# One transfer per token tile for the query and key scratch, reversed bias rows without copies, and a table chain cut into pieces

## The chip, the cores and the metric

The kernel runs on one core of one Trainium2 chip. The metric is the device time of one execution in microseconds. Three runs of the kernel before took 4225.74, 4232.83 and 4234.1 us; the median is 4232.83 us.

## What is computed

A sequence of 1024 tokens of width 1024 goes through two blocks in float32. The first block has two hybrid layers, the second one even layer and one odd layer, each followed by a wide MLP and a gated embedding step. Only the parts below touch the change:

```python
def hybrid_layer(x, c, layer_idx, ...):          # twice
    h = rms_norm(x, norm_g) * (1.0 + scale) + shift
    proj = h @ w_in                              # MLA latents, na q/k/v, diff q/k/v, gates
    o_mla = blocked_attention(q, k, v_mla, ...)  # 6 heads, 1024 x 1024 scores
    o_na = neighborhood_attention(qn, kn, vn, na_rpb, ...)   # 6 heads of 64, window 8 x 16, bias table
    o_d = blocked_diff_attention(qd, kd, vd, lam, ...)       # 4 heads, two score maps of 32 each
    return x + gate * (concat(o_mla * silu(g), ...) @ w_out)

def even_mixer(h, ...):                          # once
    q, k, v = split(rms_norm_2(h, ln) @ w_in)
    sb = stick_breaking_attention(q, k, v)       # 8 heads of 64, causal
    s5 = s5_mixer(u, ...)                        # state-space scan; needs tables of exp, cos, sin, powers
    return concat(s5, sb) @ w_out
```

## The kernel before

The program is a list of stages. Each stage has items (mostly one per token tile of 128 tokens, or one per query tile of a head) and a list `prep` of steps that are called, evenly spread, between the items of the stage ahead of it (`Net.run`, L186). A planner then orders the instructions of each engine by its own simulation of time; the order of one engine's queue is fixed after that.

**Stages of a hybrid layer**, in order: `lat`, `gate1`, `gate0`, `dv`, `dqk`, `nq`, `nk`, `nv` (projections by weight columns), then 4 stages of differential attention (`diff`), 6 of neighbourhood attention (`na`), 6 of MLA, then `out0` and `out1`. In the profile, layer 0 has `dv` to `nv` at 246 to 483 us, diff at 483 to 625, na at 625 to 730; layer 1 has them at 1165 to 1350, 1350 to 1491 and 1491 to 1597. The even layer follows `out1` of layer 1 with stages `v0`, `u`, `v1`, `q0`, `q1`, `k0`, `k1`, `glu`, and stick-breaking attention (`sb`, 8 heads) at 2189 to 2371 us.

**All data transfers are issued by SyncE's one queue** (`dma`, L243 to L249), in its order. Each issue takes one of eight completion lanes in turn, and an issue waits until the transfer that had its lane eight issues earlier has landed, as well as for the SBUF page that it writes.

**SBUF** is a pool of 43 pages of 4 KB per partition (`page`) and 10 half pages (`half`). A tile's slot is free when its last reader is done.

**Queries and keys go through DRAM.** `head_turn` (L512) transposes a token tile to features on partitions, splits it into a high and a low part on ScalarE and VectorE, and stores it into scratch laid out per head with the high rows above the low rows (`nq [6, 128, S]`, `dq [8, 64, S]`). For each group, each head of a 128-row block and each of the two parts it issues one transfer: 16 for a token tile of `dqk`, 4 for one of `nq`, `nk`, `sbq`, `sbk`. Later the attention stages load a head: `nqA`, `nqB` twice 64 rows each (L940 to L945, L1575 to L1579), `nkS` 128 rows, `dqT` four times 32 rows, `dkT` twice 64 rows (L1027 to L1033). A row is 1024 floats, 4 KB, and each loaded tile is 128 rows, 512 KB.

**The bias of the neighbourhood attention** (`na_bias`, L920): a zero-filled table `R` of 17 rows of 127 per head is written, the 15 x 31 biases are put into it, and the table is copied 64 times into `E` (3238.5 KB). The copy reads with the pattern 6 heads, 64 repeats, 2159 floats. `na_stages` (L951) then reads a Toeplitz tile `Bt` out of the copies, and GpSimd subtracts it from a mask (L961).

**The tables of the state-space mixer** (`s5_tables`, L1181): 8 steps of small VectorE instructions on 128 x 16 tiles, then 4 groups of 5 steps (`step_m` ... `step_k`) which make and store the large tables. The 8 steps and the first group stand in the prep of `out1` of layer 1, so they run beside `out0`; the other three groups stand in the preps of `v0`, `u` and `v1`.

**The modulation rows of the next layer** (`ada_steps`, L417) are made beside `dqk` to `nv` of layer 0: 32 loads of 512 KB, products on VectorE (L433), and a matmul per half row (L447).

Of the kernel before, what the change touches and what calls it, by code (L numbers as in the profile page):

```python
# [161 lines left out]
class Net:  # L162
# [23 lines left out]
    def run(self, stages):  # L186
# [18 lines left out]
        while self.active:  # L205
            self.step(None)

# [413 lines left out]
    def qk_item(self, t, hT, W, cols, heads, dst):  # L621

        def f():
# [15 lines left out]
            self.head_turn(x.rearrange("p h d -> p (h d)"), t, [hd[0:3] for hd in heads], dst)  # L639
# [32 lines left out]
    def project1(self, i, hT, early=None):  # L672
# [4 lines left out]
            "nq": [6, 128, S], "nk": [6, 128, S], "nv": [NT, 128, 768],  # L677
            "dq": [8, 64, S], "dk": [8, 64, S], "dv": [NT, 128, 256], "g": [8, 128, S]}.items()}
# [58 lines left out]
        stages.append(Stage([gains2] + W.steps(), qk(W, 512, heads((0, 8, 32, "dq", True), (256, 8, 32, "dk", True)), [D["dq"], D["dk"]]), "dqk"))  # L737
        W = self.weights(w_in[:, 416:800], 384)
        stages.append(Stage(W.steps(), qk(W, 384, heads((0, 6, 64, "nq", False)), [D["nq"]]), "nq"))
        W = self.weights(w_in[:, 800:1184], 384)  # L740
        stages.append(Stage(W.steps(), qk(W, 384, heads((0, 6, 64, "nk", False)), [D["nk"]]), "nk"))
# [3 lines left out]


# [173 lines left out]
    def na_bias(self, i):  # L920


        R = self.scratch([6, 17, 127], name=f"rpb{i}")
        E = self.scratch([6, 64, 17 * 127], name=f"rpe{i}")

        def f():
            z = self.half(F32, (128, 128), name="rz")
            self.nc.gpsimd.memset(z, 0.0)
            self.dma(R.rearrange("h j x -> (h j) x"), z[0:102, 0:127])
            self.dma(R[:, 1:16, 48:79], self.I["na_rpb"][i])  # L930
            r = R[:]
            src = bass.AP(tensor=r.tensor, offset=r.offset, ap=[[17 * 127, 6], [0, 64], [1, 17 * 127]])
            self.dma(E, src)
        return f, E

    def na_stages(self, D, mixT, E):
        nc = self.nc

        def loads(h, T):
            def q():  # L940
                T["a"] = self.page(F32R, (128, S), name="nqA")
                T["b"] = self.page(F32R, (128, S), name="nqB")
                for e in range(2):
                    self.dma(T["a"][e * 64:e * 64 + 64], D["nq"][h, 0:64])
                    self.dma(T["b"][e * 64:e * 64 + 64], D["nq"][h, 64:128])  # L945

            def k():
                T["k"] = self.page(F32R, (128, S), name="nkS")
                self.dma(T["k"], D["nk"][h])

            def b():  # L951
                Bt = T["Bt"] = self.page(F32, (128, 16, 64), name="Bt")
                r = E[:]
                for e in range(2):
                    self.dma(Bt[e * 64:e * 64 + 64], bass.AP(
                        tensor=r.tensor, offset=r.offset + h * 64 * 2159 + (1 - e) * 127 + 63,
                        ap=[[2158, 64], [127, 16], [1, 64]]))
# [45 lines left out]
    def diff_stages(self, i, D, mixT):  # L1003
# [101 lines left out]
    def block1(self):  # L1105
# [34 lines left out]
        for i in range(2):  # L1140
# [3 lines left out]
            st[3].prep.append(nf)  # L1144
# [36 lines left out]
    def s5_tables(self, T):  # L1181
# [56 lines left out]
        def exact_exp(out, x):  # L1238
# [6 lines left out]
            V.tensor_scalar_mul(out, v("r"), 1.0 / 5040)  # L1245
            for c in (1.0 / 720, 1.0 / 120, 1.0 / 24, 1.0 / 6, 0.5, 1.0):
                V.scalar_tensor_tensor(out, out, c, v("r"), op0=ALU.add, op1=ALU.mult)
            V.tensor_scalar(v("n"), v("n"), 127.0, 8388608.0, op0=ALU.add, op1=ALU.mult)
# [12 lines left out]
        def circle():  # L1261
            exact_exp(v("dt"), v("ldt"))
# [5 lines left out]
            V.scalar_tensor_tensor(v("r"), v("n"), -7.54978995489188216e-8, v("r"), op0=ALU.mult, op1=ALU.add)  # L1268
            V.tensor_mul(v("r2"), v("r"), v("r"))
# [678 lines left out]
```

## Time and profile before

| | us |
|---|---|
| median of three runs | 4232.83 |
| the profiled execution | 4231.62 |
| its span, first to last instruction | 4229.8 |
| TensorE busy | 3939.2 (93%) |
| VectorE busy | 2611.0 (62%) |
| ScalarE busy | 1815.3 (43%) |
| GpSimd busy | 1829.0 (43%) |
| differential attention, both layers | 142 + 141 |
| neighbourhood attention, both layers | 105 + 106 |
| stick-breaking attention | 182 |

The profile is of one execution. A stretch is read by the busy time of each engine in it, by the TensorE clock that was granted, and by the share of time for which the 16 DMA engines were busy. SyncE issues only, so it never counts as busy; what it does is read from its own timeline.

### The profile page before, as it was taken

Reading aid. Unit: us, or ns where it says so; the run is one execution under the profiler, and the core shown is the slowest. Engines: PE = TensorE matmul, PEld = TensorE weight load, DVE = VectorE, ACT = ScalarE, POOL = GpSimd, SP = SyncE. Lnnn points to the kernel's source line nnn. Section 1 sums busy time; section 2 is a strip of 40 time slices with the busy share of each in tenths; the row PEclk is TensorE's granted clock in tenths of the full one; section 3 lists DMA queues with packets and bytes.
Section 4 is the critical chain, followed back from the end, with each engine's and each line's share of the span. In section 5 each row is a group of like instructions: output and inputs, shape, how many; then the busy total and the mean of one; then the engine's idle time right before and its main releaser. Section 6 shows DMA issues by size and latency. Waiting matters only on the chain.

```text
span 4229.8 us, 60207 instructions
## 1 busy us (share of the span) xinstructions
PE 3939.2 (93%) x21519; PEld 3360.2 (79%) x21519; DVE 2611.0 (62%) x5073; ACT 1815.3 (43%) x3819; POOL 1829.0 (43%) x1512
## 2 busy tenths in 40 slices
PE   7996889999998899989987899999999899999999
PEld 6875658989887579878876778888888878888879
DVE  6766678846654788883669644454566744455573
ACT  5632478745534787522355331111126621111145
POOL 3432376454432774602336534444433244444432
PEclk9998999999999999999888999999999999999999
DMA  5454725332537353335453311111111111111111
GB/s 176 143 210 125 205 61 148 92 117 94 172 112 191 75 132 102 117 133 169 126 143 86 105 40 48 48 50 55 45 50 51 46 45 45 50 51 55 55 40 56
DMA packets 383549, 408.78 MB, mean 97 GB/s; under 512 B 75619, under 2 KB 311811, under 8 KB 382482
## 3 DMA queue, kind: packets, MB, share of 16 engines
q1 hardware_dynamic: 383250, 404.93, 32.5%
q8 instruction: 171, 2.80, 0.3%
q14 instruction: 128, 1.05, 0.1%
HBM read 302.86 MB, written 108.62 MB: 97 GB/s over the span
## 4 chain that ended last, share of the span: by engine, by line
PE 66%; DVE 10%; POOL 4%; ACT 4%; issue 3%; DMA 1%; SPq 0%; POOLq 0%; DVEq 0%; ACTq 0%
PE S L258 29%; PE mm L258 14%; PE tp L258 8%; PE tp L776 3%; PE mm L798 3%; PE S L914 3%; PE mm L802 1%; POOL P L761 1%; DVE P L753 1%; DVE sba L1610 1%; DVE PTl L267 1%; PE tp L337 1%; POOL wl L263 1%; PE S L1040 1%; POOL P L1612 1%
## 5 line engine op out<-in xcount | busy, mean ns | idle before, releaser
L263 POOL TENSOR_TENSOR wl<-wr,wh 128x1024 fp32r<-128x1024 f32 (+4 forms) x262 | 605.5, 2317 | 1283.0 <-ACT wh L262 822.6
L258 PE MATMUL S<-hT,wh 128*128 128x512 f32 x2176 | 688.5, 390 | 2.8 <-DVE h L1860 1.1
L1730 DVE TENSOR_TENSOR h<-h,mm 128x512 f32<-128x512 f32 x512 | 351.8, 687 | 514.8 <-PE mm L258 514.6
L258 PE MATMUL S<-wh,hT 128*128 128x256 f32 (+3 forms) x2304 | 567.9, 331 | 28.2 <-ACT vst L654 16.3
L262 ACT CAST wh<-wr 128x1024 fp32r<-128x1024 f32 (+4 forms) x264 | 262.4, 1000 | 512.7 <-PE tp L258 245.8
L258 PEld LDWEIGHTS S<-hT,wh 128*128 128x128 f32 x2176 | 407.7, 188 | 89.5 <-ACT hT L266 1.5
L1730 DVE TENSOR_TENSOR h<-h,tp 128x512 f32<-128x512 f32 x512 | 351.8, 687 | 164.7 <-PE tp L258 164.7
L258 PEld LDWEIGHTS S<-wh,hT 128*128 128x128 f32 x2304 | 411.5, 197 | 43.7 <-ACT vst L654 17.4
L258 PE MATMUL S<-hT,wl 128*128 128x512 f32 x1088 | 423.8, 389 | 1.2 <-POOL wl L263 1.1
L258 PE MATMUL S<-wl,hT 128*128 128x256 f32 (+3 forms) x1152 | 378.1, 328 | 0.7 <-POOL wl L263 0.7
L1714 ACT ACTIVATE z<-S 128x512 f32<-128x512 f32 x128 | 69.6, 596 | 634.1 <-PE S L258 634.1
L776 PE MATMUL tp<-c,P 128*128 128x128 f32 x2000 | 299.2, 286 | 36.4 <-POOL P L1612 17.1
L761 POOL TENSOR_SCALAR P<-P,sx 128x1024 f32<-128x1024 f32 (+2 forms) x232 | 232.4, 1007 | 193.7 <-DVE sx L757 90.2
L776 PEld LDWEIGHTS tp<-c,P 128*128 128x128 f32 x2000 | 240.8, 146 | 85.3 <-POOL P L1612 21.2
L267 DVE TENSOR_TENSOR PTl<-tp,PTh 128x512 fp32r<-128x512 f32 (+3 forms) x432 | 251.2, 607 | 72.3 <-ACT PTh L266 67.9
L753 DVE CUSTOM_DVE_ANT_1 P<-S,zero 128x1024 f32<-128x1024 f32 x224 | 266.8, 1216 | 32.8 <-PE S L1040 31.4
L756 ACT ACTIVATE P<-P,sx 128x1024 f32<-128x1024 f32 x224 | 258.6, 1159 | 49.6 <-DVE sx L753 36.6
L266 ACT CAST PTh<-tp 128x512 fp32r<-128x512 f32 (+3 forms) x432 | 215.2, 528 | 110.7 <-PE tp L776 104.0
L258 PE MATMUL S<-wh,mx 128*128 128x512 f32 x768 | 243.5, 394 | 3.3 <-POOL mx L819 2.6
L258 PEld LDWEIGHTS S<-hT,wl 128*128 128x128 f32 x1088 | 204.2, 188 | 44.1 <-POOL wl L263 2.0
L258 PEld LDWEIGHTS S<-wl,hT 128*128 128x128 f32 x1152 | 227.2, 197 | 6.3 <-POOL wl L263 1.0
L258 PE MATMUL mm<-wh,hT 128*128 128x256 f32 x1152 | 221.6, 285 | 2.1 <-DVE hT L267 1.7
(604 smaller groups left out, 9350.5 us busy)
## 6 DMA issues: line engine op xcount, KB each, us to landing
wr<-in_w_mlp_up_dram SPq DMA_DIRECT2D x64, 512.0 KB
wr<-in_w_mlp_down_dram SPq DMA_DIRECT2D x64, 512.0 KB
adw<-in_ada_w_dram SPq DMA_DIRECT2D x48, 512.0 KB
h<-h SPq DMA_DIRECT2D x32, 512.0 KB
wr<-in_w_in_dram SPq DMA_DIRECT2D x28, 512.0 KB
wr<-in_w_in_dram SPq DMA_DIRECT2D x24, 384.0 KB
mqT<-mq SPq DMA_DIRECT2D x24, 384.0 KB
mkT<-mk SPq DMA_DIRECT2D x24, 384.0 KB
```

The source lines that it names most:

```text
L258: self.nc.tensor.matmul(ps, a, b, start=(i == 0), stop=(i == n - 1))
L262: self.nc.scalar.copy(hi, src)
L263: (eng or self.nc.gpsimd).tensor_sub(lo, src, hi.bitcast(F32))
L266: self.nc.scalar.copy(hi, ps)
L267: self.nc.vector.tensor_sub(lo, ps, hi.bitcast(F32))
L753: nc.vector.tensor_tensor_reduce(P.rearrange("p (a b) -> p a b", a=2), Sv, self.zero.unsqueeze(2).to_broadcast([128, 2, 512]), 1.0, 3.0e38 ...
L756: nc.scalar.activation(P, P, AF.Exp, bias=nm[:, 0:1], scale=-1.0, accum_out=nm[:, 1:2])
L761: self.nc.gpsimd.tensor_scalar(P, P, f, g, op0=ALU.mult, op1=ALU.mult)
L776: self.nc.tensor.transpose(tp[:, j, :], P[:, b * 128:b * 128 + 128], self.eye)
L798: self.nc.tensor.matmul(*m, start=(j == 0), stop=(j == len(mms) - 1))
L914: nc.tensor.matmul(sp[:, c, :], T["mq", a][0:96, qs], T["mk", b][0:96, c * 512:c * 512 + 512], start=(j == 0), stop=(j == 2))
L1730: nc.vector.tensor_add(H[t][:, sl], H[t][:, sl], o)
```

## The change

1. `head_turn` stores a whole token tile with one transfer. The scratch is laid out part first: `[2, n, 128, S]` (part, block of 128 feature rows, row, token). `dq` and `dk` share one scratch `dqk [2, 4, 128, S]`.
2. A new helper `head_rows` loads a head's tile of 128 rows. Its source pattern leads with a dimension of 2 that steps from part to part (or by 0, where the same part is wanted twice). There is one transfer of 128 rows for a head of 64, and two of 64 rows for a head of 32.
3. The bias rows are reversed by a small GpSimd instruction and written to `R`; the 64 copies are gone, `Br` is read out of `R` with overlapping rows, and the subtraction reads it reversed into a page of its own.
4. The 8 table steps of the state-space mixer become 51 pieces that are mixed into the preps of `dqk`, `nq`, `nk` and `nv` of layer 1; the first group of large tables moves to the prep of the first diff stage, the second to `out1`, the third to `v1` and the fourth to `q0`.

```diff
-    def head_turn(self, x, t, groups, dst):
-        n = sum(nh * d for _, nh, d in groups) // 128
+    def head_turn(self, x, t, n, dst):
...
-        o = self.page(F32R, (128, 2, 4, 128), name="hT_")
-        self.split_ps(o[:, 0, 0:n, :], o[:, 1, 0:n, :], p[:, 0:n, :])
-        for (c0, nh, d), dd in zip(groups, dst):
-            per, b0, nb = 128 // d, c0 // 128, nh * d // 128
-            dv = dd.rearrange("(n e) (w r) s -> e w r n s", e=per, w=2)[..., t * 128:t * 128 + 128]
-            for e in range(per):
-                for w in range(2):
-                    self.dma(dv[e, w], o[e * d:e * d + d, w, b0:b0 + nb, :])
+        o = self.page(F32R, (128, 2, n, 128), name="xT")
+        self.split_ps(o[:, 0], o[:, 1], p[:, 0:n, :])
+        self.dma(dst[:, :, :, t * 128:t * 128 + 128].rearrange("w n p s -> p (w n) s"), o.rearrange("p w n s -> p (w n) s"))
...
-            "nq": [6, 128, S], "nk": [6, 128, S], "nv": [NT, 128, 768],
-            "dq": [8, 64, S], "dk": [8, 64, S], "dv": [NT, 128, 256], "g": [8, 128, S]}.items()}
+            "nq": [2, 3, 128, S], "nk": [2, 3, 128, S], "nv": [NT, 128, 768],
+            "dqk": [2, 4, 128, S], "dv": [NT, 128, 256], "g": [8, 128, S]}.items()}
...
+    def head_rows(self, src, h, d, ws, name):
+        x = self.page(F32R, (128, S), name=name)
+        per = 128 // d
+        v = src[0, h // per, h % per * d:h % per * d + d, :]
+        step = src.ap[0][0]
+        for j in range(0, len(ws), 2):
+            self.dma(x[j * d:j * d + 2 * d], bass.AP(
+                tensor=v.tensor, offset=v.offset + step * ws[j], ap=[[step * (ws[j + 1] - ws[j]), 2]] + [list(q) for q in v.ap]))
+        return x
...
-            self.dma(R[:, 1:16, 48:79], self.I["na_rpb"][i])
-            r = R[:]
-            src = bass.AP(tensor=r.tensor, offset=r.offset, ap=[[17 * 127, 6], [0, 64], [1, 17 * 127]])
-            self.dma(E, src)
-        return f, E
+            x = self.half(F32, (128, 2, 31), name="rz")[0:90]
+            self.dma(x[:, 0, :], self.I["na_rpb"][i].rearrange("h j x -> (h j) x"))
+            self.nc.gpsimd.tensor_scalar(x[:, 1, :], x[:, 0, ::-1], 1.0, 0.0, op0=ALU.mult, op1=ALU.add)
+            self.rrow = x
+        def g():
+            self.dma(R[:, 1:16, 48:79], self.rrow[:, 1, :])
+        return [f, g], R
...
-                T["a"] = self.page(F32R, (128, S), name="nqA")
-                T["b"] = self.page(F32R, (128, S), name="nqB")
-                for e in range(2):
-                    self.dma(T["a"][e * 64:e * 64 + 64], D["nq"][h, 0:64])
-                    self.dma(T["b"][e * 64:e * 64 + 64], D["nq"][h, 64:128])
+                T["a"], T["b"] = [self.head_rows(D["nq"], h, 64, w, n) for w, n in (((0, 0), "nqA"), ((1, 1), "nqB"))]
...
-                T["k"] = self.page(F32R, (128, S), name="nkS")
-                self.dma(T["k"], D["nk"][h])
+                T["k"] = self.head_rows(D["nk"], h, 64, (0, 1), "nkS")
...
-                Bt = T["Bt"]
-                nc.gpsimd.tensor_sub(Bt, self.nam.unsqueeze(1).to_broadcast([128, 16, 64]), Bt)
+                Bt = T["Bt"] = self.page(F32, (128, 16, 64), name="Bt")
+                nc.gpsimd.tensor_sub(Bt, self.nam.unsqueeze(1).to_broadcast([128, 16, 64]), T.pop("Br")[:, :, ::-1])
...
-                q = T["q", s] = self.page(F32R, (128, S), name="dqT")
-                k = T["k", s] = self.page(F32R, (128, S), name="dkT")
-                for e in range(2):
-                    self.dma(q[e * 32:e * 32 + 32], D["dq"][2 * h + s, 0:32])
-                    self.dma(q[64 + e * 32:96 + e * 32], D["dq"][2 * h + s, 32:64])
-                    self.dma(k[e * 64:e * 64 + 64], D["dk"][2 * h + s])
+                T["q", s] = self.head_rows(D["dqk"], 2 * h + s, 32, (0, 0, 1, 1), "dqT")
+                T["k", s] = self.head_rows(D["dqk"], 8 + 2 * h + s, 32, (0, 1, 0, 1), "dkT")
...
+                for j in range(4):
+                    st[4 + j].prep = self.mixed(st[4 + j].prep, tb[j * len(tb) // 4:(j + 1) * len(tb) // 4])
+                df[0].prep += steps[0]
...
-                so[1].prep += tb + steps[0]
-                self.s5_later = [("v0", steps[1]), ("u", steps[2]), ("v1", steps[3])]
+                so[1].prep += steps[1]
+                self.s5_later = [("v1", steps[2]), ("q0", steps[3])]
...
-        out = [load, turn, turn_c, circle, powers, bbar, turns, apowers]
+        def parts():
+            for part in (circle, powers, bbar, turns, apowers):
+                yield from part()
+                yield
+        gen = parts()
+        out = [load, turn, turn_c] + [lambda: next(gen, None) for _ in range(47)] + [lambda: [None for _ in gen]]
```

The stick-breaking stages load `nqA`, `nqB` and `nkS` with `head_rows` in the same way.

## Rows read from the trace of the kernel before

**Rows 1.** The page: busy time, share of the span, instructions; shares of the last chain.

```profile
PE 3939.2 (93%) x21519; PEld 3360.2 (79%) x21519; DVE 2611.0 (62%) x5073; ACT 1815.3 (43%) x3819; POOL 1829.0 (43%) x1512
...
PE 66%; DVE 10%; POOL 4%; ACT 4%; issue 3%; DMA 1%; SPq 0%; POOLq 0%; DVEq 0%; ACTq 0%
```

**Rows 2.** Windows: stretch, length, busy PE, PEld, DVE, ACT, POOL, clock, DMA share, GB/s.

```profile
246.00:290.00 44.00, 34.48 (x182) 29.01 (x181) 23.28 (x26) 16.88 (x33) 18.74 (x8) 0.88 0.97 344
349.00:404.00 55.00, 19.12 (x114) 18.21 (x112) 25.46 (x37) 10.46 (x25) 9.84 (x7) 0.72 0.46 137
...
1165.00:1180.00 15.00, 8.26 (x51) 7.85 (x49) 4.58 (x10) 7.46 (x14) 5.16 (x3) 0.77 1.03 321
1250.00:1290.00 40.00, 33.43 (x174) 31.79 (x172) 16.00 (x41) 12.84 (x33) 13.24 (x10) 0.87 0.36 90
...
1785.00:1825.00 40.00, 29.61 (x142) 24.38 (x141) 39.11 (x268) 1.44 (x3) 0.00 (x0) 0.81 0.20 65
```

**Rows 3.** Windows of the diff, na and sb attention stretches, same columns.

```profile
483.00:625.00 142.00, 121.27 (x547) 76.28 (x546) 110.88 (x211) 107.16 (x195) 108.35 (x70) 0.90 0.41 106
625.00:730.00 105.00, 98.41 (x686) 83.26 (x685) 81.76 (x224) 86.52 (x199) 69.38 (x79) 0.98 0.56 144
...
1350.00:1491.00 141.00, 118.21 (x540) 73.95 (x538) 108.20 (x208) 105.85 (x192) 106.68 (x69) 0.94 0.43 111
1491.00:1597.00 106.00, 99.44 (x701) 84.16 (x701) 85.30 (x228) 88.52 (x203) 71.36 (x81) 1.00 0.57 144
...
2189.00:2371.00 182.00, 134.44 (x803) 117.43 (x802) 168.82 (x212) 103.81 (x194) 126.56 (x132) 0.85 0.38 95
```

**Rows 4.** DMA issues by tile: count and size of one.

```profile
dqT<-dq SPq DMA_DIRECT2D x64, 128.0 KB
...
rpe<-rpb SPq DMA_DIRECT2D x2, 3238.5 KB
...
nkS<-nk SPq DMA_DIRECT2D x12, 512.0 KB
```

**Rows 5.** Windows: wide loads, the bias copy twice, and mixed traffic; columns as above.

```profile
10.00:30.00 20.00, 19.59 (x54) 12.57 (x55) 14.46 (x14) 12.94 (x13) 0.00 (x0) 1.00 1.02 407
...
1144.00:1148.00 4.00, 4.00 (x23) 3.34 (x22) 2.91 (x9) 2.56 (x8) 0.00 (x0) 1.00 0.36 147
1148.00:1152.00 4.00, 4.00 (x19) 3.33 (x18) 3.73 (x6) 1.12 (x3) 3.54 (x5) 1.00 0.37 158
...
490.00:530.00 40.00, 34.20 (x153) 21.06 (x152) 34.52 (x67) 30.89 (x56) 34.78 (x23) 0.93 0.70 178
```

**Rows 6.** Timeline of SyncE's queue: start, length of the issue in us, what, count.

```profile
223.45 9.49 SPq L248 DMA_DIRECT2D mk<-mTl  x1
232.99 8.39 SPq L248 DMA_DIRECT2D g<-gate  x1
...
337.85 3.67 SPq L248 DMA_DIRECT2D dq<-hT__3260  x8
...
1330.68 1.00 SPq L248 DMA_DIRECT2D dqT<-dq  x2
```

**Rows 7.** Issues of one tile on SyncE: ns min/median/max, first and last start.

```profile
L248 SPq DMA_DIRECT2D dqT<-dq x64: 302/419/1147, 452.9 to 1393.4; - x64
...
L248 SPq DMA_DIRECT2D nqA<-sbq x16: 450/587/3278, 2169.8 to 2313.1; - x16
L248 SPq DMA_DIRECT2D nq<-hT__3563 x4: 592/603/636, 382.4 to 384.5; - x4
```

**Rows 8.** Waits by total: waiting engine and line, releaser, us, times, longest.

```profile
PE mm L447 <- DVE acc L442: 38.8, 3, 32.9
...
PE S L258 <- ACT vst L654: 16.3, 4, 8.6
```

**Rows 9.** Waits of SyncE's own queue.

```profile
SPq L248 <- PE tp L776: 198.6, 45, 12.2
```

**Rows 10.** One line's instructions: ns min/median/max, first and last start.

```profile
L961 POOL TENSOR_TENSOR Bt<-c,Bt x12: 2375/2400/3316, 589.8 to 1574.1; 128x1024 f32<-128x1024 f32 x12
...
L1240 DVE TENSOR_SCALAR s5s<-s5s x2: 174/7391/14608, 1767.9 to 1786.8; 128x16 f32<-128x16 f32 x2
```

More of the change, by code (lines that the diff above doesn't have):

```diff
@@ L206, in run, with mixed @@
             self.step(None)
+    @staticmethod
+    def mixed(a, b):
+        k = sorted([((j + 0.5) / len(a), 0, j) for j in range(len(a))] + [((j + 0.5) / len(b), 1, j) for j in range(len(b))])
+        return [(a, b)[w][j] for _, w, j in k]
     def note(self, tag, t):
@@ L638, in f @@
             yield
-            self.head_turn(x.rearrange("p h d -> p (h d)"), t, [hd[0:3] for hd in heads], dst)
+            self.head_turn(x.rearrange("p h d -> p (h d)"), t, nall * d // 128, dst)
         return f
@@ L736, in project1 @@
         W = self.weights(w_in[:, 1568:2080], 512)
-        stages.append(Stage([gains2] + W.steps(), qk(W, 512, heads((0, 8, 32, "dq", True), (256, 8, 32, "dk", True)), [D["dq"], D["dk"]]), "dqk"))
+        stages.append(Stage([gains2] + W.steps(), qk(W, 512, heads((0, 8, 32, "dq", True), (256, 8, 32, "dk", True)), D["dqk"]), "dqk"))
         W = self.weights(w_in[:, 416:800], 384)
-        stages.append(Stage(W.steps(), qk(W, 384, heads((0, 6, 64, "nq", False)), [D["nq"]]), "nq"))
+        stages.append(Stage(W.steps(), qk(W, 384, heads((0, 6, 64, "nq", False)), D["nq"]), "nq"))
         W = self.weights(w_in[:, 800:1184], 384)
-        stages.append(Stage(W.steps(), qk(W, 384, heads((0, 6, 64, "nk", False)), [D["nk"]]), "nk"))
+        stages.append(Stage(W.steps(), qk(W, 384, heads((0, 6, 64, "nk", False)), D["nk"]), "nk"))
         W = self.weights(w_in[:, 1184:1568], 384)
@@ L923, in na_bias @@
         R = self.scratch([6, 17, 127], name=f"rpb{i}")
-        E = self.scratch([6, 64, 17 * 127], name=f"rpe{i}")
         def f():
@@ L1143, in block1 @@
             nf, E = self.na_bias(i)
-            st[3].prep.append(nf)
+            st[3].prep += nf
             stages += st
@@ L1261, in circle @@
         def circle():
-            exact_exp(v("dt"), v("ldt"))
+            yield from exact_exp(v("dt"), v("ldt"))
+            yield
             V.tensor_mul(v("th"), v("li"), v("dt"))
@@ L1268, in circle @@
             V.scalar_tensor_tensor(v("r"), v("n"), -7.54978995489188216e-8, v("r"), op0=ALU.mult, op1=ALU.add)
+            yield
             V.tensor_mul(v("r2"), v("r"), v("r"))
@@ L1271, in circle @@
             V.scalar_tensor_tensor(v("s"), v("s"), 1.0, v("r"), op0=ALU.add, op1=ALU.mult)
+            yield
             horner(v("c"), v("r2"), (-1.0 / 3628800, 1.0 / 40320, -1.0 / 720, 1.0 / 24, -0.5))
             V.tensor_scalar_add(v("c"), v("c"), 1.0)
+            yield
             V.tensor_scalar(v("q"), v("n"), -1.5, 0.25, op0=ALU.add, op1=ALU.mult)
@@ L1282, in circle @@
             V.tensor_scalar(v("even"), v("odd"), -1.0, 1.0, op0=ALU.mult, op1=ALU.add)
+            yield
             for out, a, b, op in (("sin", "s", "c", ALU.add), ("cos", "c", "s", ALU.subtract)):
@@ L1305, in powers @@
             V.tensor_mul(v("x2"), v("lr"), v("dt"))
-            exact_exp(v("mag"), v("x2"))
+            yield from exact_exp(v("mag"), v("x2"))
+            yield
             V.tensor_mul(v("ar"), v("mag"), v("cos"))
@@ L1312, in powers @@
             V.tensor_mul(rho, rho, rho)
+            yield
             square(v("p0r"), v("p0i"), v("cos"), v("sin"))
@@ L1316, in powers @@
             square(v("p0r"), v("p0i"), v("p0r"), v("p0i"))
+            yield
             unit(v("p0r"), v("p0i"))
             for m in range(1, 7):
+                yield
                 square(v(f"p{m}r"), v(f"p{m}i"), v(f"p{m - 1}r"), v(f"p{m - 1}i"))
@@ L1340, in bbar @@
             V.tensor_mul(v("fr"), v("fr"), v("den"))
+            yield
             V.tensor_mul(v("fi"), v("ai"), v("lr"))
@@ L1344, in bbar @@
             V.tensor_mul(v("fi"), v("fi"), v("den"))
+            yield
             B = P["B"] = P["bc"][:, 0]
@@ L1356, in grow @@
                 cmul(V, e[:, 0, :, m:2 * m], e[:, 1, :, m:2 * m], e[:, 0, :, 0:m], e[:, 1, :, 0:m], y[0], y[1], [w[:, 0, :, 0:m], w[:, 1, :, 0:m]])
+                yield
         def turns():
@@ L1365, in turns @@
                 V.memset(x[:, 1, :, 0:1], 0.0)
-            grow(e, w, 16, "p", 0)
-            grow(f, w, 8, "p", 4)
+            yield
+            yield from grow(e, w, 16, "p", 0)
+            yield from grow(f, w, 8, "p", 4)
         def apowers():
@@ L1376, in apowers @@
                 cmul(V, e[:, 0, :, m + 1], e[:, 1, :, m + 1], e[:, 0, :, m], e[:, 1, :, m], v("ar"), v("ai"), [w[:, 0], w[:, 1]])
+                yield
         def outer(s, out, x, y, op_r, op_i, order):
@@ L1574, in q @@
             def q():
-                T["a"] = self.page(F32R, (128, S), name="nqA")
-                T["b"] = self.page(F32R, (128, S), name="nqB")
-                for e in range(2):
-                    self.dma(T["a"][e * 64:e * 64 + 64], D["q", h // 4][h % 4, 0:64])
-                    self.dma(T["b"][e * 64:e * 64 + 64], D["q", h // 4][h % 4, 64:128])
+                T["a"], T["b"] = [self.head_rows(D["q", h // 4], h % 4, 64, w, n) for w, n in (((0, 0), "nqA"), ((1, 1), "nqB"))]
             def k():
-                T["k"] = self.page(F32R, (128, S), name="nkS")
-                self.dma(T["k"], D["k", h // 4][h % 4])
+                T["k"] = self.head_rows(D["k", h // 4], h % 4, 64, (0, 1), "nkS")
             return [q, k]
@@ L1622, in even_stages @@
         w_in = I["w_in_even_2"][0]
-        D = {(x, c): self.scratch([4, 128, S], name=f"sb{x}{c}") for x in "qk" for c in range(2)}
+        D = {(x, c): self.scratch([2, 2, 128, S], name=f"sb{x}{c}") for x in "qk" for c in range(2)}
         D["v"] = self.scratch([NT, 128, 1024], name="sbv")
@@ L1638, in mk @@
             def mk(t):
-                return lambda: self.qk_item(t, hT, W, 256, [(0, 4, 64, L[key], False)], [D[key, c]])()
+                return lambda: self.qk_item(t, hT, W, 256, [(0, 4, 64, L[key], False)], D[key, c])()
             return [mk(t) for t in range(NT)]
```

9 lines of the change are left out of this document (5 added, 4 removed).

## The prediction

> **What bounds the kernel now.** I read the page first: TensorE is busy 93% of the span and carries 66% of the last chain; no DMA, no queue and no other engine comes near [rows 1]. So an edit pays only where TensorE idles, and costs wherever it opens a new gap. The windows show the gaps near the edits [rows 2]: 35.9 of 55 us idle at 349:404 (clock 0.72), 9.5 of 44 at 246:290, 6.7 of 15 at 1165:1180, 6.6 of 40 at 1250:1290, 10.4 of 40 at 1785:1825. Then the three attentions that read the new scratch [rows 3]: diff 142 and 141 us, na 105 and 106, sb 182. They are full for TensorE or VectorE, and DMA is at 0.38 to 0.57 of sixteen engines. That spare DMA time is the cover under which every head's queries and keys are loaded, and it is what I test the change against.
>
> **Stores.** A `dqk` token tile now takes 16 issues; eight of them fill 3.67 us of SyncE, 0.46 us each [rows 6], and one of `nq` takes 0.60 us [rows 7]. Per layer 128 + 64 issues go to 24, about 59 + 38 us of queue time down to 11. What stood behind them is paid only where TensorE waited:
> - The modulation row at 371 us: TensorE waits 32.9 us for a VectorE sum [rows 8] whose 512 KB loads queue among these stores. VectorE, pages and DMA bandwidth stay, so I take two thirds of the idle 35.9 us: **-24** (0 to -36).
> - 1250:1290 in layer 1: **-5** (0 to -7).
> - sb's stores: no wait of TensorE's behind them is in my rows; nothing.
>
> **Bias copy.** After `rpe<-rpb` the next two issues block SyncE for 9.49 and 8.39 us [rows 6], and TensorE's projections wait for `vst` tiles, whose stores stand in that queue: 16.3 us over four waits, 8.6 the longest [rows 8]. Without the copies I take **-14** (0 to -16). New are a 90 x 31 GpSimd instruction and a reversed read in the subtraction. The latter took 2.4 us forward [rows 10]; reversed it may take anything from that to double, 12 x 2.4 = 29 us in all, on a GpSimd that is busy 69 of 105 us [rows 3] and a head ahead: nothing, and up to 2.4 us per layer if the first head's is late. `Br` beside `Bt` takes one page more per head.
>
> **Table chain.** In 1785:1825 VectorE is busy 39.1 of 40 us on it while TensorE idles 10.4 us at a clock of 0.81 [rows 2]. Moved into `dqk` to `nk`, where VectorE has 24 of 40 us free (1250:1290) and the pieces are under 1 us each, the head norms behind a piece lose about that much. One first instruction took 14.6 us for no reason that a row tells [rows 10]; if that recurs among the head norms it eats the gain. **-14** (0 to -16). Its loads and 11 stores move to SyncE's queue at `dqk` and `nv`; three of its pages stay allocated through the attentions.
>
> Gains together: -57 (-14, the copies alone, to -75).
>
> **Loads: the term that decides.** Before, `dqT` came as four transfers of 32 rows, `nkS` as one of 128 rows [rows 4]; the source patterns led with 32, 64 or 128. Now each leads with 2. What a short leading dimension does is seen in the bias copy, whose source leads with 6: while it runs nearly alone the DMA share is 0.36 and 0.37, that is 6/16 = 0.375, at 147 and 158 GB/s; loads with 128 leading rows fill the share to 1.02 at 407 GB/s [rows 5]. Both are 25 GB/s per busy engine (147/(16 x 0.36) = 25.5; 407/(16 x 1.02) = 24.9). I read it as: as many engines as the leading dimension has room for. With 2 that is two engines, and a 512 KB tile costs 262,144 B / 25 GB/s = **10.5 us** of both. Bounds: 10.3 (25.5 GB/s) and 16.5 (0.70 at 178 GB/s, 15.9 each [rows 5], but that traffic holds rows of 256 and 512 B, these are 4 KB rows as in the first); I take the near end, and 13 as the price that I still think likely.
>
> That SyncE sat 9.49 us on the issue behind the copy [rows 6] speaks for one line in which such loads stand behind each other. No row shows two of them in flight. The Trainium skill, "DMA: Bandwidth & Descriptors", section "Why a DMA increments its semaphore by 16 and not by 1", says that the engine count is the largest number up to 16 that divides both patterns' slowest dimensions, and that SyncE's transfers use the lowest-numbered engines; the trace agrees on the count for 6 (0.36 to 0.37). By its second half all these loads would queue on one pair, +367 as below; if each took another pair it would be the third rival's +30.
>
> Sum per stretch, loads in a stream, with the pair's share of the wide transfers (per diff head some 0.5 MB: 1.5 us; na 1.3 MB: 5; sb 0.5 MB: 2):
> - diff head: 4 x 10.5 + 1.5 = 43.5, four heads 174, against 35 us per head now. na head: 3 x 10.5 + 5 = 36.5, six heads 219, against 17.5. sb head: 33.5, eight heads 268, against 22.8.
> - Layer 0: the first issue is at 452.9 [rows 7]; 452.9 + 174 + 219 + the last head's compute 17.5 = 863, where na ends at 730 now: **+133**. Layer 1 from 1330.7 [rows 6]: 1741 against 1597: **+144**. sb from 2169.8 [rows 7]: 2461 against 2371: **+90**. Together +367.
> - SyncE waits for pages that TensorE frees (`SPq <- PE tp L776`, 45 times [rows 9]); where the next na head's first load waits for the present head's compute, the pair runs dry for some 4 us a head: **+50** for both layers (0 to +100).
>
> Queued behind a narrow load on SyncE stand the `nv` and `nk` stores, `V`, gates, and everything eight issues later by its lane; TensorE waits for these only through the loads already counted. That SyncE does block behind a copy on few engines is seen in the 9.49 us issue [rows 6].
>
> 4231.6 (profiled execution) + 367 + 50 - 57 = **4592 us**. The profiled execution is 1.2 us under the median of three, which I ignore.
>
> **Rivals.**
> 1. *The clock falls in the gaps as well.* Granted 0.72 where TensorE idled most [rows 2]. At half clock diff's busy time would be 121.3 x 0.90/0.5 = 218 us, over the stream's 174 (layer 1: 118.2 x 0.94/0.5 = 222); na's 193 and sb's 228 stay under. +92: 4684. Against: TensorE would be busy 0.7 of the time in diff, and sb ran at 0.85 with that share [rows 3].
> 2. *The pattern isn't carried as written* and the loads use all sixteen engines: in each part the 64 (or 32) rows are one contiguous run, and contiguous runs do load wide now. Then only the gains are left: 4231.6 - 57 = 4175, faster. For it: `nkS` lands in time today. Against: the bias copy also reads contiguous rows and kept its 6. It decides once the share in na stays near 0.5 and the stage near 105 us.
> 3. *Each narrow load gets another pair.* Up to eight in flight then hide each other, and only the first head of the five or so unhidden starts waits some 6 us longer: 4231.6 - 57 + 30 = 4205, faster. Against: SyncE sat 9.49 us on one issue behind the copy [rows 6] while the share left ten of sixteen engines idle [rows 5], so a queue in order doesn't flow around a narrow transfer.
>
> **How the numbers follow.** Forecast 0.79, rival 1 0.08, rival 2 0.08, rival 3 0.03, and 0.02 for gains and costs that cancel. Predicted: 4592. Low end: the wide transfers' share hidden in the other engines' time (-12 -60 -16 = -88), no page lag (-50), full gains (-18): 4436. High end: 92 loads at 13 instead of 10.5 us (+230), lag +50: 4872; with all at 16.5 it would be over 5200, which I leave out, as I do rivals 2 and 3. Range 4430 to 4870, rival 1 within. Faster by over 0.2% 0.11, within 0.2% 0.02, slower 0.87; 0.2% is the spread of the runs before and about what can be told from no change.
>
> **What would show it.** Right: in na and sb windows a DMA share near 2/16 = 0.125 with TensorE idle, waits of the score matmuls (L977, L1040, L1594) on the `nq`, `dqk`, `sbq` loads, long issues on SyncE; na near 230 us, diff near 175, sb near 270, and no 9 us issue after the bias rows. Gains: under 15 us idle at the modulation row; `out0` of layer 1 as short as layer 0's. Wrong: if the attentions keep their lengths, the leading 2 doesn't confine the loads, and all of the +417 is void; if they grow by twice as much, the price per row was 16.5, not 10.5.

## The result, and the profile after

The changed kernel takes 4518.09 us (median; 4515.83 to 4521.76), the kernel before 4230.95 us beside it: a ratio of 1.068, 95% interval 1.066 to 1.070. It is slower by 287 us. The forecast was 4592 us, range 4430 to 4870. The profiled execution took 4517.0 us, with a span of 4515.1 us at a mean granted clock of 0.935 (before 0.965).

The page of the changed kernel, the same lines as [rows 1]: busy time, share of the span and instructions of each engine, then the shares of the last chain.

```profile
PE 3966.7 (88%) x21519; PEld 3380.7 (75%) x21519; DVE 2606.3 (58%) x5073; ACT 1815.2 (40%) x3819; POOL 1816.5 (40%) x1514
...
PE 49%; DMA 8%; DVE 4%; issue 2%; ACT 2%; POOL 2%; SPq 1%; POOLq 0%; DVEq 0%; ACTq 0%
```

TensorE does the same 21519 matmuls, but transfers, 1% of the chain before, now carry 8% of it. The waits by total (waiting engine and line, releaser, us, times, longest) say which ones:

```profile
PE S L985 <- DMA nkS<-nk: 128.5, 8, 21.0
...
PE S L1617 <- DMA nkS<-sbk: 108.9, 8, 22.7
...
PE S L1044 <- DMA dkT<-dqk: 43.1, 4, 16.4
```

Before, no score matmul waited for a load in the list of waits. L985, L1617 and L1044 are the score matmuls of na, sb and diff. The windows of the attentions answer to [rows 3] (stretch, length, busy PE, PEld, DVE, ACT, POOL, clock, DMA share, GB/s); the last three are short pieces of the first na:

```profile
433.00:616.00 183.00, 126.70 (x561) 77.86 (x560) 104.30 (x211) 110.51 (x200) 108.46 (x71) 0.84 0.24 81
616.00:815.00 199.00, 105.01 (x675) 90.56 (x673) 82.74 (x222) 84.92 (x194) 65.19 (x78) 0.75 0.30 86
...
2403.00:2654.00 251.00, 134.06 (x794) 117.33 (x795) 162.62 (x207) 99.52 (x189) 113.16 (x129) 0.76 0.20 68
620.00:630.00 10.00, 8.53 (x55) 6.46 (x53) 5.45 (x14) 7.30 (x16) 10.00 (x8) 1.00 0.13 51
655.00:670.00 15.00, 14.78 (x85) 10.90 (x84) 7.84 (x21) 9.27 (x22) 2.84 (x4) 0.91 0.13 52
640.00:650.00 10.00, 0.00 (x0) 0.00 (x0) 0.00 (x0) 0.00 (x0) 0.00 (x0) 0.50 0.28 79
```

The stages are 41, 94 and 69 us longer with the same work in them. Where only head loads are in flight the DMA share is 0.13, two of sixteen engines (0.125), at 51 to 52 GB/s, some 25 GB/s per engine; and in 640:650 no engine computes at all. The queue that issues it all, SyncE's timeline (start, length of the issue in us, what), shows the loads of one na head:

```profile
579.31 0.92 SPq L254 DMA_DIRECT2D nqA<-nq  x1
580.33 0.80 SPq L254 DMA_DIRECT2D nqB<-nq  x1
581.22 8.63 SPq L254 DMA_DIRECT2D nkS<-nk  x1
589.94 9.67 SPq L254 DMA_DIRECT2D V<-nv  x1
599.78 10.86 SPq L254 DMA_DIRECT2D gt<-g  x1
610.74 4.33 SPq L254 DMA_DIRECT2D Br<-rpb  x2
615.16 3.29 SPq L254 DMA_DIRECT2D nqA<-nq  x1
```

From one head's `nqA` to the next are 35.9 us here, and (761.2 - 579.3)/5 = 36.4 us on average over the stage. SyncE is held for some 10 us each on the issues of the wide `V` and `gt`, which stand behind the narrow loads. At the modulation row, where 35.9 of 55 us were idle [rows 2], and at the `nv` stage of layer 1, where TensorE was busy for 52.0 of 52 us (1298:1350) before:

```profile
354.00:410.00 56.00, 51.23 (x294) 47.32 (x294) 36.99 (x74) 19.79 (x56) 10.81 (x7) 0.99 0.58 186
...
1400.00:1450.00 50.00, 25.63 (x138) 24.86 (x137) 17.00 (x39) 5.99 (x18) 0.00 (x0) 0.73 0.44 155
```

The first lost its gap; the second has 24 us of a new one. TensorE waits there for `vst`, the tile that the `nv` store sends, and SyncE sits on the `nk` and `nv` stores behind the first diff loads; where the loads are wide (rows first, below) each of these stores but one is issued in under 1 us.

```profile
PE S L264 <- DVE vst L273: 24.4, 2, 14.4
```

```profile
1416.95 5.75 SPq L254 DMA_DIRECT2D nk<-xT  x1
1422.80 8.33 SPq L254 DMA_DIRECT2D nv<-vst  x2
```

The whole, cut at the first instruction of a stage on TensorE. "Rows first" is the first experiment below, the changed kernel with wide loads; its column splits the 287 us into gains and costs.

| us | before | changed | rows first |
|---|---|---|---|
| start to the first head transposition of layer 0 | 304.8 | 291.2 | 294.8 |
| `dqk` to `nv`, layer 0 | 177.8 | 141.7 | 130.8 |
| diff, layer 0 | 142.9 | 183.2 | 140.0 |
| na, layer 0 | 104.8 | 199.0 | 111.8 |
| MLA and output, layer 0 | 280.6 | 282.3 | 280.6 |
| `lat` to the first head transposition, layer 1 | 207.7 | 201.1 | 203.4 |
| `dqk` to `nv`, layer 1 | 131.8 | 156.5 | 132.9 |
| diff, layer 1 | 140.7 | 164.5 | 141.0 |
| na, layer 1 | 105.3 | 197.3 | 108.6 |
| MLA, output, even layer to sb | 592.6 | 586.1 | 575.9 |
| sb and its output | 314.5 | 385.4 | 313.6 |
| the rest (MLPs) | 1726.2 | 1726.9 | 1727.5 |

### The profile page after: what moved, and what is told of

Same layout as the page of the kernel before. It is cut to its first block, busy times and chain, and to the rows that moved or that the text cites. A ratio compares the mean times of both kernels' runs of the same rounds, so it can differ in the third digit from the quotient of the medians.

```text
span 4515.1 us, 59379 instructions
## 1 busy us (share of the span) xinstructions
PE 3966.7 (88%) x21519; PEld 3380.7 (75%) x21519; DVE 2606.3 (58%) x5073; ACT 1815.2 (40%) x3819; POOL 1816.5 (40%) x1514
## 4 chain that ended last, share of the span: by engine, by line
PE 49%; DMA 8%; DVE 4%; issue 2%; ACT 2%; POOL 2%; SPq 1%; POOLq 0%; DVEq 0%; ACTq 0%
PE S L264 22%; PE mm L264 12%; PE tp L264 8%; DMA nkS<-sbk 4%; DMA nkS<-nk 3%; PE S L925 1%; PE mm L809 1%; PE tp L787 1%; SPq L254 1%; DMA dkT<-dqk 1%; PE S L1547 1%; PE tp L343 1%; DVE P L764 1%; DVE xn L332 0%; PE mm L813 0%
## 5 line engine op out<-in xcount | busy, mean ns | idle before, releaser
L809 PE MATMUL mm<-PTh,V 128*128 128x256 f32 (+1 forms) x784 | 213.0, 299 | 11.5 <-ACT PTh L272 5.5
```

What stands on the lines that cost most here:

```text
L809: self.nc.tensor.matmul(*m, start=(j == 0), stop=(j == len(mms) - 1))
```

## The experiments

Theory: the leading 2 confines a load to two DMA engines; that is the whole loss, and the other edits gain. Rivals: the loss lies in the new layout or the other edits; or it goes by the number of narrow transfers, through what each blocks on SyncE.

### The same loads, rows first

In `head_rows`:

```diff
-                tensor=v.tensor, offset=v.offset + step * ws[j], ap=[[step * (ws[j + 1] - ws[j]), 2]] + [list(q) for q in v.ap]))
+                tensor=v.tensor, offset=v.offset + step * ws[j], ap=[list(v.ap[0]), [step * (ws[j + 1] - ws[j]), 2], list(v.ap[1])]))
```

> The changed kernel, in which every load of a query or key tile walks its source rows first and the two parts second (leading count 64 or 32 instead of 2; the rows then lie interleaved in the tile, the same way for queries and keys, and a product over all 128 rows doesn't mind). Number of issues, bytes, layout, stores, bias rows and table chain stay as in the changed kernel. Theory (two engines per load are the whole loss): na back to 105 us, diff to 140, sb to 180 or less, DMA share in na near 0.5, and only the gains are left: 4231 less 57 (the prediction's) to 115 (what the starts of the three streams in the changed kernel show) = 4116 to 4174 us. Rival (the loss lies in the new layout, the pages of Br, the pieces of the chain or SyncE's order, whatever the engines): above 4400 us, with na still over 150 us.

Measured: 4161.25 us, ratio to before 0.983 (0.980 to 0.986); a second time (with the wide copy, below) 4160.63, 0.9836 (0.9823 to 0.9849). Exchanging two entries of a pattern takes back the whole loss: (1.0681 - 0.9836) x 4231 = 357 us. The windows of diff and na of layer 0 and of sb:

```profile
426.00:566.00 140.00, 121.62 (x563) 75.32 (x562) 105.14 (x212) 110.17 (x200) 108.93 (x72) 0.94 0.36 94
566.00:677.00 111.00, 97.20 (x669) 81.87 (x669) 81.79 (x220) 82.88 (x192) 64.18 (x77) 0.98 0.45 133
...
2120.00:2298.00 178.00, 134.93 (x795) 117.25 (x794) 166.15 (x208) 101.47 (x192) 124.38 (x131) 0.84 0.26 83
```

The engines do the same work as in the changed kernel; in na TensorE's idle time falls from 94 to 14 us, and at a clock of 0.98 for 0.75 its busy time from 105.0 to 97.2. The trace also records the updates (events) by which a transfer reports its shares as done. Counted per load, with the median time from issue to landing:

```
                        events   nqA     nqB     nkS    (us, na)
changed (leads with 2)     3    14.8    23.3    33.6
leads with 4 (below)       5     8.0    11.8    14.9
rows first (64)           16     3.8     4.4     4.0
```

(Loads that lead with 4 are half tiles of 64 rows.) Three, five and sixteen events stand beside two, four and sixteen engines (where fewer than sixteen work, one event more than engines, and it comes as the issue ends; the restored bias copies below, led by 6, leave seven). In the changed kernel the three tiles of an na head, issued within 2 to 5 us, land 10.2 to 12.1 us apart, one behind the other: one pair of engines serves all in turn. The layout as cause falls: the layout is the same here.

### One load per part

```diff
-        for j in range(0, len(ws), 2):
-            self.dma(x[j * d:j * d + 2 * d], bass.AP(
-                tensor=v.tensor, offset=v.offset + step * ws[j], ap=[[step * (ws[j + 1] - ws[j]), 2]] + [list(q) for q in v.ap]))
+        for j in range(len(ws)):
+            self.dma(x[j * d:j * d + d], bass.AP(
+                tensor=v.tensor, offset=v.offset + step * ws[j], ap=[list(q) for q in v.ap]))
```

> The changed kernel, with one load for each part of a tile (64 or 32 rows, the part's own contiguous rows, no leading 2), so twice as many issues as in the changed kernel and no interleaving. Theory: as wide as the kernel with rows first, 4116 to 4180 us; the 92 x 1 to 2 further issues of 0.5 us lie beside other work. Rival (one transfer per tile was itself worth something, or the issues are on the path): 20 us or more above the kernel with rows first. Rival (loss not from the leading 2): above 4400 us.

Measured: 4181.71 us, 0.988 (0.984 to 0.991), some 20 us above rows first by the medians, 1.7 us above the theory's range and at the edge of the rival's 20. Diff is 145.8 and 145.3 us against 140.0 and 141.0, sb 181.3 against 178.1; against the second execution of rows first (143.1, 140.2 and 180.6) it is less. The two intervals overlap, so a price of the 124 further issues is hinted at and not shown. The loads are wide and the large loss is gone, so again it was the leading 2.

### Narrow keys only

As the kernel with one load per part, but `nkS` and `dkT` keep the leading 2.

```diff
+        if name[1] == "q" or name == "nqB":
+            for j in range(len(ws)):
+                self.dma(x[j * d:j * d + d], bass.AP(
+                    tensor=v.tensor, offset=v.offset + step * ws[j], ap=[list(q) for q in v.ap]))
+            return x
```

> The kernel with one load per part, but key tiles (nkS, dkT) loaded with the leading 2 as in the changed kernel: 36 of its 92 narrow tiles. Theory (a stream of two engines costs only what it is longer than the head's own work): one tile of 10.5 us in an na or sb head (17.5 and 22.8 us of work), two in a diff head (21 of 35 us), so all hidden, and only the first head of a stage waits: 0 to 40 us above the kernel with one load per part. Rival (each narrow load costs what it blocks on SyncE behind it, so the cost goes by their number): 36/92 of the 399 us that the changed kernel's attentions lost, 156 us above it.

Measured: 4214.51 us, 0.995 (0.993 to 0.997): 33 us above its control (one load per part), inside the theory's 0 to 40 and far from the rival's 156. (The rival's 399 us stands in no run; with the 357 us that the loads cost in all it would be 140.) na of layer 0 is 110.7 us, the control 110.6: a narrow tile of 10 us per head beside 17.5 us of work costs nothing. The cost sits in diff (160.3 and 152.2 against 145.8 and 145.3) and `dqk` to `nv` of layer 1 (142.1 against 134.4), where the stream starts: TensorE's waits there are put down to an `nv` store (9.4 us) and `V` (7.7) in diff of layer 0, and to a `vst` tile (11.4) in the projections of layer 1. na of layer 1 is 3.7 us longer. Narrow loads don't cost by their number.

### The kernel before with narrow queries

```diff
-                for e in range(2):
-                    self.dma(T["a"][e * 64:e * 64 + 64], D["nq"][h, 0:64])
-                    self.dma(T["b"][e * 64:e * 64 + 64], D["nq"][h, 64:128])
+                for w, x in enumerate("ab"):
+                    v = D["nq"][h, w * 64:w * 64 + 64]
+                    self.dma(T[x], bass.AP(tensor=v.tensor, offset=v.offset, ap=[[0, 2]] + [list(p) for p in v.ap]))
```

and so for `sbq`; for `dqT` two transfers of 64 rows with the same `[0, 2]`.

> The kernel before, with its query tiles alone loaded by a source pattern that leads with 2 (step 0: the same rows twice); layout, stores, keys, bias copies and chain as before. Theory: na head 2 x 10.5 + 5 + 1.3 = 27.3 us against 17.5, +59 per layer; diff head 21 + 2.8 = 24 under its 35; sb head 21 + 2 + 1.3 = 24.3 against 22.8, +12: 4231 + 118 + 12 = 4361 us (4300 to 4410). Rival (cost by number of narrow tiles, 56 of 92): 4231 + 243 = 4474 us. Rival (the loss comes from the new layout or the other edits): within 10 us of 4231.

Measured: 4371.89 us, 1.033 (1.031 to 1.036): +141 us where the theory's sum had +130. na takes 141.0 and 146.4 us, +36 and +41 (theory 59 each), diff 160.1 and 161.3, +17 and +21 (theory 0), sb 195.5, +16.5, and 7.0 more from the MLA of layer 1 to sb (theory 12 together). So the total came out nearer than its parts, by luck. na's stream ran as worked out (in layer 0 the last four key tiles land at 680.2, 709.1, 736.6 and 765.5 us, 28.4 apart, theory 27.3), but the first two heads' tiles had been loaded ahead (608.2 and 646.5, the stage begins at 640.1), and only three of the six heads show a wait of TensorE's for a load. In return diff and sb cost what the theory left out. The waits of this kernel:

```profile
PE S L977 <- DMA nkS<-nk: 65.1, 6, 14.9
...
PE S L1594 <- DMA nkS<-sbk: 43.5, 7, 15.5
...
PE S L1040 <- DMA dkT<-dk: 40.5, 3, 16.7
```

TensorE waits for key tiles, which are wide here, led by 128 or 64 rows. A wide `nkS` lands 24.8 us (median) after its issue in na, 4.0 us in the kernel with rows first. Its sixteen events show why: in each of the twelve na heads fourteen come within 4.8 to 12.3 us of the issue and the last two after 17.1 to 26.3. Two shares of sixteen stand behind the narrow tiles, and the load is complete only with them.

### Four engines

One load per part, the rows of a part taken in strides so that each load leads with 4.

```diff
-                tensor=v.tensor, offset=v.offset + step * ws[j], ap=[list(q) for q in v.ap]))
+                tensor=v.tensor, offset=v.offset + step * ws[j], ap=[[rs, 4], [rs * 4, d // 4], list(v.ap[1])]))
```

(`rs` is the row stride; queries and keys are permuted alike.)

> The kernel with one load per part (4182 us), the rows of each part taken in strides so that every load leads with 4: four engines, by the price of the prediction 100 GB/s, 262 KB in 2.6 us, a 512 KB tile in 5.2 us. Theory: na head 3 x 5.25 + 5 = 20.7 us against 17.5, +39 for both layers; diff head 22.5 under 35, sb head 17.8 under 22.8; near 4220 (4180 to 4270), DMA share in na at 0.3 to 0.5. Rival (narrow costs something whatever the count, once under 16): half of the changed kernel's loss or more, over 4350. Rival (4 is enough, the price falls faster than the count): 4182.

Measured: 4192.29 us, 0.992 (0.990 to 0.993), 6 us above its control by the spans (4190.4 against 4184.8), 18 by the ratios. The windows of both na stages, and of the first in the control:

```profile
573.00:692.00 119.00, 104.98 (x687) 88.77 (x685) 81.52 (x223) 86.56 (x198) 61.76 (x77) 0.93 0.46 126
1454.00:1574.00 120.00, 103.21 (x686) 88.14 (x684) 81.52 (x223) 86.20 (x197) 61.68 (x76) 0.93 0.47 126
```

```profile
571.00:682.00 111.00, 99.92 (x688) 84.12 (x687) 81.36 (x223) 85.65 (x198) 62.39 (x77) 0.98 0.55 135
```

na grows by 8.3 and 7.4 us, diff and sb by 2.2 at most; 9.0 us of that come back between the MLA of layer 1 and sb (570.1 us for 579.1), a stretch that also differs by 5.0 us between the two executions of rows first. The stage takes 118.9/6 = 19.8 us a head, where 3 x 5.25 + 5 = 20.7 was worked out, but that mean counts heads loaded ahead: the last three key tiles of a layer land 22 to 23 us apart, and in both layers the scores of the last two heads start within 0.2 us of that landing. In the last four heads of a layer twelve events of `V` come within 5.2 us of its issue and four after 10.2 to 17.3 us: four shares of sixteen are late here, as two were above. Twice the engines leave a small part of the loss, as a stream that just passes the head's work must.

### What the gains are worth: stores

Rows first, but with a token tile's old transfers into the new scratch:

```diff
-        self.dma(dst[:, :, :, t * 128:t * 128 + 128].rearrange("w n p s -> p (w n) s"), o.rearrange("p w n s -> p (w n) s"))
+        for c0, nh, d in groups:
+            b0, nb = c0 // 128, nh * d // 128
+            for e in range(128 // d):
+                for w in range(2):
+                    self.dma(dst[w, b0:b0 + nb, e * d:e * d + d, t * 128:t * 128 + 128].rearrange("n p s -> p n s"), o[e * d:e * d + d, w, b0:b0 + nb, :])
```

> The kernel with rows first, but each token tile of queries and keys stored in as many transfers as before (16 for dqk, 4 for nq, nk and sb). The prediction gave the stores 29 us (24 at the modulation row, 5 in layer 1; 0 to 43): this kernel 29 us above the one with rows first, near 4190, 24 of it before the first diff attention of layer 0, with TensorE idle at the modulation row. By what the kernel with rows first gained before that point (57 us, of which the copies can be 10 at most) it would be near 45: 4205. Rival (the idle time at the modulation row came from VectorE or the pages): under 10 us.

Measured: 4217.89 us, 0.997 (0.996 to 0.998): 0.0133 x 4231 = 56 us above rows first, more than the 29 and the 45 expected. `dqk` to `nv` of layer 0 takes 179.8 us against 130.8 (+49), of layer 1 139.0 against 132.9 (+6). This kernel in `dqk` to `nv` of layer 0, and its wait there:

```profile
296.00:476.00 180.00, 134.38 (x719) 121.88 (x718) 103.55 (x206) 47.46 (x129) 33.13 (x27) 0.88 0.53 153
```

```profile
PE mm L453 <- DVE acc L448: 35.7, 3, 30.3
```

And rows first in the same stage:

```profile
295.00:426.00 131.00, 126.48 (x718) 117.67 (x716) 98.40 (x206) 48.52 (x130) 35.51 (x26) 1.00 0.71 218
```

In the kernel before the stage read the same:

```profile
305.00:483.00 178.00, 130.35 (x719) 117.97 (x716) 102.07 (x205) 47.76 (x130) 33.17 (x26) 0.89 0.52 148
```

The modulation row's wait returns with the stores, VectorE's work being the same, so it came with the store transfers in the queue, not from VectorE or the pages by themselves. Without them the idle time of the whole stage falls from 45.6 to 4.5 us and the clock is 1.00 in place of 0.88, which takes 7.9 us off the busy time.

### What the gains are worth: bias copies

Rows first, with the table of 64 copies as before the change (the reversal and `Br` go, and the tile is read forward; only the copy is shown):

```diff
+            src = bass.AP(tensor=r.tensor, offset=r.offset, ap=[[17 * 127, 6], [0, 64], [1, 17 * 127]])
+            self.dma(E, src)
```

> The kernel with rows first (the changed kernel with wide loads), but the bias rows kept as before: the table of 64 copies written once per layer from a pattern that leads with 6, the tile read forward, no Br. The prediction gave the copies 14 us for both layers (0 to 16): this kernel 14 us above the one with rows first, near 4175; the two 8 to 9 us issues behind the copy come back in the nv stages (TensorE idle in a run of some 8 us, layer 0 and 1 together 10 to 16 us). Rival (with the shorter queue nothing waits behind the copy): 0. Rival (the reversed read and Br cost the na stages 10 us, which the kernel with rows first shows over before: 111.8 and 108.6 against 104.8 and 105.4): na back to 105 and 105, and the kernel within 5 us of the one with rows first or under it.

Measured: 4174.86 us, 0.987 (0.986 to 0.989): 14 us above rows first, as expected, but as the sum of two things. The stretches before the head transpositions grow by 8.1 us in layer 0 (the `vst` wait of 8.6 us is back) and 13.4 in layer 1, where TensorE waits for a load of the table chain, now behind the copy:

```profile
PE tp L1230 <- DMA s5r<-in_s_lambda_re_dram: 11.8, 1, 11.8
```

In return na takes 104.4 and 107.5 us, against 111.8 and 108.6 with the reversed rows. The reversed subtraction itself is no slower, a median of 2382 ns for 2400 before [rows 10]. What else in the new bias path costs 7.4 us in one na and 1.1 in the other (`Br`'s page, an order of instructions) is open; ScalarE waits for that subtraction six times in rows first, 6.5 us in all, and with the copies restored not once.

A wide copy tells whether the bytes or the engines held the queue:

```diff
-            src = bass.AP(tensor=r.tensor, offset=r.offset, ap=[[17 * 127, 6], [0, 64], [1, 17 * 127]])
-            self.dma(E, src)
+            src = bass.AP(tensor=r.tensor, offset=r.offset, ap=[[0, 64], [17 * 127, 6], [1, 17 * 127]])
+            self.dma(E.rearrange("h c x -> c h x"), src)
```

> The kernel with rows first and the 64 copies of the bias rows restored, but the copy written from a pattern that leads with the 64 copies instead of the 6 heads; the bytes are the same. Theory (the 8.6 and 11.8 us gaps behind the copy come from its six engines): the copy takes 6/16 of its time, both gaps shrink below 4 us, and na, whose tile is then read forward from one page, keeps its 104 and 107 us (111.8 and 108.6 with reversed rows): 4174.9 less some 8 + 11 = about 4155, at or under the kernel with rows first. Rival (the 6.6 MB of the copy block the queue whatever its pattern): 4175, gaps unchanged.

> The kernel with rows first again, beside the one with the wide copy, so that the two share their runs of the kernel before: 4155 to 4167 us.

Measured: 4153.95 us, 0.9824 (0.9811 to 0.9838), beside 4160.63 for rows first. The copy lands 14.1 and 13.8 us after its issue instead of 24.8 and 24.7 (not in 6/16 of it, which would be 9.3), leaves sixteen events instead of seven, and with all 64 copies written the two waits shrink from 8.6 and 11.8 us to 1.3 and 0.5; na takes 106.0 and 107.6 us. The longest issue behind it, copies by 6 and then by 64:

```profile
222.19 9.18 SPq L254 DMA_DIRECT2D mk<-mTl  x1
231.42 8.39 SPq L254 DMA_DIRECT2D g<-gate  x1
```

```profile
225.70 6.55 SPq L254 DMA_DIRECT2D g<-gate  x1
```

Two long issues became one, in layer 1 too (8.85 and 8.58 us, then 5.33). Both this kernel and rows first beat the kernel before and the changed one; between the two the intervals overlap.

### What the gains are worth: table chain

Rows first, with the chain in one stretch ahead of the second output stage (the 51 pieces are its 8 steps again, not shown):

```diff
-                for j in range(4):
-                    st[4 + j].prep = self.mixed(st[4 + j].prep, tb[j * len(tb) // 4:(j + 1) * len(tb) // 4])
-                df[0].prep += steps[0]
...
-                so[1].prep += steps[1]
-                self.s5_later = [("v1", steps[2]), ("q0", steps[3])]
+                so[1].prep += tb + steps[0]
+                self.s5_later = [("v0", steps[1]), ("u", steps[2]), ("v1", steps[3])]
```

> The kernel with rows first, but the table chain in one stretch ahead of the second output stage, as before. The prediction gave the spreading 14 us (0 to 16): this kernel 14 us above the one with rows first, near 4175, with the layer 1 output stage longer by what it gains in the projections (dqk to nv of layer 1). Rival (the spreading only moves the time into layer 1's projections, which the changed kernel lengthened by 18 us): within 5 us of the kernel with rows first, its projections some 15 us shorter. Rival (spreading also frees na or sb): more than 25 us.

Measured: 4159.86 us, 0.984 (0.983 to 0.986): no difference from rows first that can be told. The windows of `dqk` to `nv` of layer 1 and of the output stages, in this kernel and then in rows first:

```profile
1161.00:1281.00 120.00, 120.00 (x705) 117.10 (x705) 68.27 (x180) 47.98 (x127) 34.18 (x26) 1.00 0.58 167
1687.00:1800.00 113.00, 100.05 (x507) 82.80 (x506) 90.75 (x359) 23.40 (x45) 32.44 (x18) 0.92 0.41 141
```

```profile
1161.00:1294.00 133.00, 126.04 (x745) 121.11 (x744) 99.62 (x297) 48.96 (x130) 35.38 (x26) 0.99 0.54 159
1697.00:1800.00 103.00, 99.10 (x501) 82.61 (x501) 44.87 (x74) 27.94 (x56) 37.32 (x20) 0.98 0.39 131
```

The wait that the spreading removes from the output stages stands in this kernel's list:

```profile
PE tp L1434 <- DVE s5M L1408: 9.7, 1, 9.7
```

From the first matmul of the output stages to sb, spreading gives 10.9 us (16.0 against the second execution of rows first); it takes 12.9 us in the projections, which run with TensorE 120.0 of 120 us busy when the chain is not in them. The rival holds: the time moved.

## Why the prediction was right, point by point

**The deciding term** held by its mechanism and its price. Two engines (share 0.13), 25 GB/s each (51 to 52 GB/s together), 36.4 us a head in na where 36.5 was worked out, and (2584.6 - 2365.5)/7 = 31.3 in sb for 33.5. The cost of the loads is the changed kernel less rows first: layer 0 (`dqk` to na) 10.9 + 43.2 + 87.2 = 141 us for the predicted 133; layer 1 23.6 + 23.5 + 88.7 = 136 for 144; sb and the stretch ahead of it 82 for 90. Together 359, predicted 367. The Trainium skill's rule ("DMA: Bandwidth & Descriptors", section "Why a DMA increments its semaphore by 16 and not by 1") on the number of engines agrees with 2, 4, 6 and 16 here; its lowest-numbered engines agree with loads that land one after the other, though no run shows which engines these are.

**The page lag** (+50) failed. The stream was taken to run dry for 4 us per na head; at 36.4 us a head it didn't. In layer 0 the last shares follow each other without a hole: `nkS` at 615.1 us, `V` 617.3, `gt` 618.6, `Br` 619.3 and 620.3, and the next `nqA` at 630.7, 10.4 us later. So na came out at 199 and 197 us, not near the 230 of the prediction's signs. By the sums above this is most of the 74 us by which 4592 was too high.

**Where the loss shows** was right in total and shifted in place. The stream's first issue was put at 452.9 us, its place before; with the stores gone it came at 392.8. And "TensorE waits for these only through the loads already counted" was wrong: narrow diff loads held the `nk` and `nv` stores back, and `dqk` to `nv` became 10.9 and 23.6 us longer.

**Stores** (-29) were under-sized: 49 + 6 us. The step that failed is "two thirds of the idle 35.9 us". The window 349:404 was too short (the whole of `dqk` to `nv` had 178.0 - 130.4 = 47.6 us idle, as its row above shows) and the clock, 0.89 over that stage, wasn't counted; nor did a third have to be held back for VectorE or pages.

**Bias copies** (-14) came out at 14, from two errors that cancel: 21.5 us of queue, part of it a wait that only the spread chain makes, less the 8.5 us that na got longer by, which the prediction set at nothing. That is luck.

**Table chain** (-14) came out at 0. The step "VectorE has 24 of 40 us free" read the busy time of the window 1250:1290, in which TensorE itself had a gap; the stage as a whole is TensorE's. In rows first 40 small matmuls of the first table group came into it (3.0 us), and TensorE idles for 7.0 us, 3.3 of them for head norms and 3.1 for a `vst` tile that VectorE makes, while VectorE's busy time rises from 68.3 to 99.6 us. The gains together are 70 us for the predicted 57. Then 4231 - 70 + 357 = 4518.

**Rivals.** The clock fell, to 0.75 in na and 0.84 in diff, but TensorE's busy time in diff only from 121.6 to 126.7 us, far under the 183 us of the stage; it didn't become the bound. A pattern not carried as written, or another pair for each load, would have left na at 105 us and the share at 0.5; and behind three narrow tiles just two of the sixteen events of `V` are late (25.4 to 27.8 us after its issue, the others by 14.7), so all three were on one pair. One slip changes nothing: with every load at 16.5 us the prediction's own sum gives 5194, not over 5200.

## What to carry to other kernels

Before merging transfers, look at the slowest dimension of both patterns: a leading 2 is two DMA engines, and exchanging it with the rows, where a product over all rows doesn't mind their order, keeps the one issue and all engines. Price a load by its engines and compare the stream of a whole head with that head's work; what fits under it costs little, what doesn't is paid for every head that wasn't loaded ahead, and wide transfers behind it pay too. For the worth of a gap, read the whole stage and its clock, and before moving work into a stage, see which engine it belongs to.

## What was not expected of the hardware

A transfer over all sixteen engines that is issued behind narrow ones lands as late as they do: 24.8 us for a 512 KB key tile, against 4.0; in the changed kernel `V`, sixteen events too, took 26.8 us in na. All but two of its shares are there long before. SyncE takes 7.5 to 11 us each to issue `nkS`, `V` and `gt` behind narrow loads in na, though the data of `V` and `gt` need other engines too; what holds these issues no run shows. And 3.3 MB written by six engines held SyncE for two issues of 8.4 to 9.2 us in each layer, by sixteen for one of 6.6 and 5.3.
